# One step of a hybrid decoder layer on one core: keys and values turned by VectorE instead of TensorE, twelve gate tiles ahead of the attention, one more pair of the mixer by halves, value products moved behind the next transposes

## The chip, the cores and the metric

The kernel runs on one core of a Trainium2 chip. The metric is the device time of one execution in microseconds (us). Three executions of the kernel before took 1712.73, 1715.70 and 1717.58 us; the median is 1715.7 us. A further execution was recorded by the hardware profiler; all rows below are from that one.

## The reference, cut to what matters

One decoder layer is computed for 1024 prompt tokens and for 8 sequences of 4 new tokens each (1056 token columns together; every activation is kept transposed, features on the partitions, tokens on the free axis). All data are 32 bit floats.

- `h = RMSNorm(x)`, and one combined projection `h @ w_in` gives, among other things, the queries, keys and values of the attention (512 columns each) and the two gates `g_A` and `g_B` (1024 columns each).
- Branch A is stick-breaking attention, 8 heads of 64: `s = sigmoid(q.k/8 + bias)` under a strictly causal mask, weight `w = s * (product of 1 - s over all later keys)`, output `w @ v`.
- Branch B is a gated delta rule, 4 heads of 128, evaluated in chunks (called GDN below), a serial chain per head.
- Merge: `sigmoid(g_A) * (o_A @ w_pa) + sigmoid(g_B) * (o_B @ w_pb)`, then `w_o`, then the residual.
- Channel mixer: `x + relu(RMSNorm(x) @ w_up)^2 @ w_down`, hidden width 4096, that is 32 tiles of 128 features.
- The prompt's new keys and values are outputs too, in token order: `new_k_prompt` and `new_v_prompt`, pages of 128 tokens by 8 heads by 64.

## The kernel before, in words

A dense product is three matrix products in a fast 32 bit format: every operand is split by ScalarE and VectorE into a high and a low part, and `dense` (lines 134 to 139) issues high*high, high*low and low*high for each 128 rows of depth. A tile is 128 features by up to 288 token columns. Transposes by TensorE and the value products of the attention are issued in the full 32 bit format instead, and TensorE goes back and forth between the two.

Instructions are placed by a planner that simulates the engines: the program's order is a priority, `tc.issue_after(ins)` keeps what follows behind an instruction, `tc.high_priority()` puts it ahead. Each engine then executes its own list strictly in order. DMAs are issued from SP's list, except a few that GpSimd (POOL in the profile) or ScalarE issues; an issue waits in its engine's list until what it reads is there.

The stages, in order of time:

1. Norm and transposes of the input.
2. GDN heads (`gdn_head`), with the projections of queries, keys and values (lines 793 to 831) and the first gate tiles used by the planner as work between the steps of the serial chain. For each of four pairs of heads `p` and for keys and values, the projected tile `f` (128 features by 1024 tokens) is turned into token order by eight TensorE transposes (`tr8`, `tr` on line 111) into two PSUM banks, copied by ScalarE to `nt` (line 819) and stored by SP to the output (line 821); the values are stored a second time to the scratch tensor `v_d` (line 823). The tiles `f`, `hi`, `lo`, `nt` and later the gate tiles `gt` share four buffers (`NFT = 4`). GpSimd has steps of every GDN head: masks of `E` (lines 430, 432) and `tv` (457, 458), powers (`rpow`, line 114).
3. Attention of the 8 new-token sequences, whose cached pages are gathered by GpSimd DMAs (lines 599, 612).
4. The attention of the prompt in 64 blocks (head, 128 queries). `scores` makes a block's `s`, GpSimd masks it and forms `1 - s` (lines 951, 954), VectorE runs the scan and the product (958, 959). `stage_b` issues, four blocks later, the block's transposes (`transposed`, line 962), then some fill work, then `values_of`. For heads 0 to 5 the value product takes two blocks at once, each into one half of the partitions, and the loop over key tiles alternates between the two blocks. The first product needs the first block's weights alone. Until block 34 (`SPLIT`) the fill work is what is left of the 16 gate tiles (`gjobs`, 11 before the attention and 5 in it, four steps each) and nine steps that write a transposed copy of x (`residual_step`); after it, the product with `w_pb`.
5. Merge, `w_o`, second norm.
6. Mixer, first half. With `NF = 16`, hidden tiles `f` and `f + 16` are a pair; 13 pairs (`f` from 3) are combined to seven blocks and stored for the second half (`hc_d`), and pairs 0 to 2 are stored as they are (`h_d`). `up_products` makes a pair with seven half-depth products; `up_plain` makes one tile directly and is used for pairs 0 to 2 in the first half of the tokens.
7. Mixer, second half, in three groups of pairs, [3..6], [7..10] and [11..15] (line 1538 ff.): seven products per pair (`pw`, 168 matrix instructions a pair), each with its own split of the loaded `hc` (`load_h`) and of the weights (`weight_part`). The first group's first loads are issued by GpSimd.
8. The six plain tiles (`fl`) are multiplied directly (`pv`, 96 matrix instructions a tile), beside the final norm and the output.

## Time and profile before

| | |
|---|---|
| time, median of 3 runs | 1715.7 us (1712.73 to 1717.58) |
| the profiled execution's own time | 1713.05 us |
| its span in the trace | 1711.3 us |
| granted TensorE clock, mean | 0.997 |
| VectorE busy | 1155.2 us |
| ScalarE busy | 774.3 us |
| GpSimd busy | 207.3 us |

The span runs from the first to the last recorded instruction; 1.75 us of the execution lie around it. PE is TensorE's matrix work, PEld its weight loads, DVE VectorE, ACT ScalarE, POOL GpSimd, SP the engine that issues most DMAs. Matrix instructions are pipelined: the recorded length of one is more than its distance to the next, so the distance is read from the number of instructions in a stretch in which PE is busy throughout.

### The profile page before, as it was taken

How to read it: one execution, taken by the hardware profiler on the slowest of the kernel's cores; microseconds unless marked ns; L12 is line 12 of the kernel's file. 1: busy time of each engine (PE TensorE's matmuls, PEld its weight loads, DVE VectorE, ACT ScalarE, POOL GpSimd, SP SyncE). 2: the span in 40 equal slices, each digit the busy share in tenths (PEclk: the TensorE clock that was granted, in tenths of full speed). 3: DMA queues.
4: the chain of work that ended last, by engine and by line, in shares of the span. 5: the costliest groups of instructions: out<-in, count | busy, mean ns of one | idle time of the engine just before them, and what ended most of it. 6: DMA issues, size and time to landing. Idle time of an engine off the chain costs nothing.

```text
span 1711.3 us, 34643 instructions
## 1 busy us (share of the span) xinstructions
PE 1676.0 (98%) x13958; PEld 1620.3 (95%) x13958; DVE 1155.2 (68%) x2317; ACT 774.3 (45%) x1542; POOL 207.3 (12%) x243
## 2 busy tenths in 40 slices
PE   6999999999999999999999999999999999999998
PEld 6999999999999799988999999999999999999998
DVE  6656676877325337779766578877777679788843
ACT  5453434343324225565433356544444564444353
POOL 1110111110004225345300000000000000000000
PEclk9999999999999999999999999999999999999999
DMA  5132233244537577876134645554443766433421
GB/s 181 38 118 81 69 95 103 73 124 134 152 96 233 156 202 181 201 211 189 44 126 132 176 132 150 160 160 145 139 139 125 268 216 214 144 118 96 133 78 62
DMA packets 259036, 239.24 MB, mean 140 GB/s; under 512 B 55890, under 2 KB 217011, under 8 KB 258876
## 3 DMA queue, kind: packets, MB, share of 16 engines
q1 hardware_dynamic: 253926, 226.27, 44.0%
q0 software_dynamic: 3200, 10.52, 2.0%
q8 instruction: 110, 1.80, 0.4%
q10 hardware_dynamic: 1750, 0.23, 0.1%
q14 instruction: 50, 0.41, 0.1%
HBM read 163.21 MB, written 73.77 MB: 138 GB/s over the span
## 4 chain that ended last, share of the span: by engine, by line
PE 88%; DVE 4%; DMA 4%; issue 2%; ACT 2%; SPq 0%; POOL 0%; DVEq 0%; POOLq 0%; ACTq 0%
PE pu L139 6%; PE pu L137 6%; PE pu L138 6%; PE pw L139 5%; PE pw L138 5%; PE pw L137 5%; PE pd_g L137 4%; PE pd_g L138 4%; PE pd_g L139 4%; PE wt L111 2%; PE po L996 2%; PE px L138 1%; PE px L137 1%; PE px L139 1%; PE pv L139 1%
## 5 line engine op out<-in xcount | busy, mean ns | idle before, releaser
L139 PE MATMUL pu<-Xh,ul 128*128 128x264 f32 x812 | 230.1, 284 | 0.0
L137 PE MATMUL pu<-Xh,uh 128*128 128x264 f32 x812 | 229.8, 283 | 0.1
L138 PE MATMUL pu<-Xl,uh 128*128 128x264 f32 x812 | 229.7, 283 | 0.0
L137 PE MATMUL pw<-hc,w 128*128 128x264 f32 x728 | 204.1, 284 | 2.4 <-ACT w L1490 2.4
L138 PE MATMUL pw<-hc,w 128*128 128x264 f32 x728 | 204.6, 285 | 0.0
L139 PE MATMUL pw<-hc,w 128*128 128x264 f32 x728 | 200.8, 285 | 1.0 <-DVE w L1491 1.0
L137 PEld LDWEIGHTS pu<-Xh,uh 128*128 128x128 f32 x812 | 153.1, 189 | 0.3 <-ACT uh L1241 0.3
L138 PEld LDWEIGHTS pu<-Xl,uh 128*128 128x128 f32 x812 | 152.7, 188 | 0.0
L139 PEld LDWEIGHTS pu<-Xh,ul 128*128 128x128 f32 x812 | 152.0, 188 | 0.0
L138 PE MATMUL pd_g<-xl,wh_g 128*128 128x256 f32 (+1 forms) x512 | 149.4, 292 | 0.0
L137 PE MATMUL pd_g<-xh,wh_g 128*128 128x256 f32 (+1 forms) x512 | 149.3, 292 | 0.0
L139 PE MATMUL pd_g<-xh,wl_g 128*128 128x256 f32 (+1 forms) x512 | 148.5, 290 | 0.0
L137 PEld LDWEIGHTS pw<-hc,w 128*128 128x128 f32 x728 | 136.8, 188 | 2.6 <-ACT w L1490 2.6
L138 PEld LDWEIGHTS pw<-hc,w 128*128 128x128 f32 x728 | 136.2, 188 | 0.0
L139 PEld LDWEIGHTS pw<-hc,w 128*128 128x128 f32 x728 | 134.4, 188 | 1.4 <-DVE w L1491 1.4
L958 DVE TENSOR_TENSOR_SCAN pr<-am 128x127 f32<-128x127 f32 (+7 forms) x64 | 89.0, 1393 | 30.1 <-POOL am L954 30.1
L137 PEld LDWEIGHTS pd_g<-xh,wh_g 128*128 128x128 f32 x512 | 97.1, 190 | 3.2 <-issue 2.5
L138 PEld LDWEIGHTS pd_g<-xl,wh_g 128*128 128x128 f32 x512 | 97.1, 190 | 2.7 <-issue 2.4
L139 PEld LDWEIGHTS pd_g<-xh,wl_g 128*128 128x128 f32 x512 | 97.0, 189 | 2.0 <-issue 1.8
L1490 ACT ACTIVATE w<-a 128x512 fp32r<-128x512 f32 x78 | 43.4, 620 | 90.3 <-PE pw L139 80.1
L139 PE MATMUL px<-mh,wl_wo 128*128 128x264 f32 x256 | 72.2, 285 | 1.3 <-DVE wl_wo L1242 1.2
L138 PE MATMUL px<-ml,wh_wo 128*128 128x264 f32 x256 | 72.6, 285 | 0.0
(578 smaller groups left out, 5069.0 us busy)
## 6 DMA issues: line engine op xcount, KB each, us to landing
hc_d<-t SPq DMA_DIRECT2D x26, 924.0 KB
hc<-hc_d SPq DMA_DIRECT2D x87, 264.0 KB
a<-in_w_down_dram SPq DMA_DIRECT2D x48, 256.0 KB
ws_g<-in_w_in_dram SPq DMA_DIRECT2D x16, 512.0 KB
ws_wo<-in_w_o_dram SPq DMA_DIRECT2D x32, 256.0 KB
ua<-in_w_up_dram SPq DMA_DIRECT2D x16, 512.0 KB
ub<-in_w_up_dram SPq DMA_DIRECT2D x16, 512.0 KB
gA_d<-gt SPq DMA_DIRECT2D x8, 528.0 KB
```

Source lines behind the costliest of these rows:

```text
L111: PE.transpose(out, in_, ident[:k, :k])
L137: PE.matmul(pt[:, :n], lhsT=wh[k], rhs=xh[k], start=(k == 0), stop=False)
L138: PE.matmul(pt[:, :n], lhsT=wh[k], rhs=xl[k], start=False, stop=False)
L139: PE.matmul(pt[:, :n], lhsT=wl[k], rhs=xh[k], start=False, stop=(k == nk - 1))
L958: V.tensor_tensor_scan(pr[:, n - 1:0:-1], am_r, am_r, 1.0, op0=ALU.mult, op1=ALU.bypass)
L996: PE.matmul(po[64 * r:64 * r + 64, 0:P], lhsT=vn[:, b, rs], rhs=wts[hh, 2 * m + r][:, b * P:(b + 1) * P], start=(b == 0), stop=(b == 2 * m ...
L1490: S_.activation(tl[:, 0], src, AF.Copy)
```

## The change

- New keys and values: the transposes of TensorE and ScalarE's copies go. VectorE's `transpose` transposes every 32 by 32 square of `f` within its place (one instruction over 128 by 1024), and GpSimd issues four DMAs that put the squares where they belong in a scratch tensor `n_d` in token order: each moves 1024 pieces of 128 bytes. A fifth GpSimd DMA copies the scratch tensor to the output, 1024 pieces of 512 bytes, and has to wait for the four. `v_d` and its store go; the attention reads `n_d["v"]`.
- Gates: 12 tiles ahead of the attention instead of 11, 4 in it; a gate's weights are fetched when the split of the tile before has been issued (`fetch_w`). The nine residual steps are on consecutive fill steps, 3 to 11.
- Attention: block `x - 1`'s value product is issued behind block `x`'s last transpose instead of at the end of its own stage. `wt` has three buffers instead of two, `pr` one instead of two.
- Mixer: 14 pairs by halves (`f` from 2) and 4 plain tiles; `up_plain` makes a pair and, for pair 2, the combined blocks. The first half has as many matrix instructions as before. Groups are [2..5], [6..10] and [11..15]. The first group's first weight splits have high priority.

```diff
+    n_d = {x: dr.tile([4, NP, P], F32, name=f"n{x}_d") for x in "kv"}
...
+    ahead_w = {}
+    def fetch_w(col):
+        ahead_w[col] = wpool.tile([P, 8, P], F32, tag="wst", name=f"ws_c{col}", bufs=1)
+        SY.dma_start(ahead_w[col], winv[:, :, col:col + P])
...
-                ws.append(load_w(winv[:, :, col:col + P], name))
+                if col not in ahead_w:
+                    fetch_w(col)
+                ws.append(load_w(None, name, st=ahead_w[col]))
+                if next_col is not None:
+                    fetch_w(next_col)
...
-                for hf, pt in enumerate(tr8(f, f"n{nm}{p}", lambda n_: dtile(n_, True))):
-                    S_.activation(nt[:, hf * 512:(hf + 1) * 512], pt, AF.Copy)
+                V.transpose(nt, f[:, 0:NP])
+                for a in range(4):
+                    G.dma_start(n_d[nm][p].rearrange("(b i) f -> i b f", i=32)[:, :, 32 * a:32 * a + 32],
+                                nt[32 * a:32 * a + 32].rearrange("i (b j) -> i b j", j=32))
                 dst = nk_prompt if nm == "k" else nv_prompt
-                SY.dma_start(dst[0, 0, :, :, 2 * p:2 * p + 2, :].rearrange("c t h d -> t c (h d)"), c8(nt))
-                if nm == "v":
-                    SY.dma_start(v_d[p], c8(nt))
+                G.dma_start(dst[0, 0, :, :, 2 * p:2 * p + 2, :].rearrange("c t h d -> (c t) (h d)"), n_d[nm][p])
...
-            wts[blks[x]] = transposed(blks[x], state[x][0])
+            wts[blks[x]], last = transposed(blks[x], state[x][0])
+        if x:
+            with tc.issue_after(last.ins):
+                values_of(blks[x - 1])
         for f in fill:
             f()
-        values_of(blks[x])
+        if x == NB - 1:
+            values_of(blks[x])
...
-    for j, b in gjobs[:11]:
+    for j, b in gjobs[:12]:
...
-            if t % 2 == 1 and t >= 3:
-                fills.append(lambda t=(t - 3) // 2: residual_step(t))
+            if 3 <= t < 12:
+                fills.append(lambda t=t - 3: residual_step(t))
...
-    NPL = 3
+    NPU, NPL = 3, 2
...
-    groups = [list(range(3, 7)), list(range(7, 11)), list(range(11, 16))]
+    groups = [list(range(2, 6)), list(range(6, 11)), list(range(11, 16))]
...
-            ws = [weight_part(q, f, i) for q, f in zip(qs2, fs)]
+            with tc.high_priority() if gi == i == 0 else ExitStack():
+                ws = [weight_part(q, f, i) for q, f in zip(qs2, fs)]
```

## Rows read from the trace of the kernel before

**Rows 1.** The page: busy time of the engines, and the chain of waits by engine.
```profile
PE 1676.0 (98%) x13958; PEld 1620.3 (95%) x13958; DVE 1155.2 (68%) x2317; ACT 774.3 (45%) x1542; POOL 207.3 (12%) x243
...
PE 88%; DVE 4%; DMA 4%; issue 2%; ACT 2%; SPq 0%; POOL 0%; DVEq 0%; POOLq 0%; ACTq 0%
```

**Rows 2.** Busy time by stretch; columns as the first line names them.
```profile
core 0: us, PE busy (x) PEld busy (x) DVE busy (x) ACT busy (x) POOL busy (x), PEclk, DMA share, GB/s
160.00:460.00 300.00, 295.63 (x2702) 289.12 (x2701) 206.21 (x524) 123.04 (x293) 32.14 (x29) 1.00 0.38 113
635.00:755.00 120.00, 119.99 (x985) 108.22 (x984) 86.06 (x79) 63.13 (x139) 51.19 (x66) 1.00 0.78 183
755.00:795.00 40.00, 39.09 (x306) 32.00 (x304) 37.36 (x37) 25.16 (x50) 27.06 (x24) 1.00 0.94 278
1200.00:1220.00 20.00, 20.00 (x167) 20.00 (x166) 14.47 (x33) 9.40 (x17) 0.00 (x0) 1.00 0.46 148
```

**Rows 3.** PE, new keys and values: group by form (busy, mean ns, idle), chain pieces (start, length).
```profile
L111 PE MATMUL t_nv<-ident,vf 128*128 128x128 f32 x32 | 5.0, 278 | 0.0
L111 PE MATMUL t_nk<-ident,kf 128*128 128x128 f32 x32 | 4.9, 276 | 1.7 <-ACT ntk L819 1.7
...
23.52 0.87 PE xtp L111 x8
```

**Rows 4.** PE in order of time, value products and neighbours: start, length, instructions.
```profile
640.11 0.43 PE L996 MATMUL po<-wt,vn 128*64 128x128 f32 x2
...
708.78 0.43 PE L996 MATMUL po<-wt,vn 128*64 128x128 f32 x2
709.15 0.39 PE L138 MATMUL pd_g<-xl,wh_g 128*128 128x256 f32 x1
...
849.53 1.09 PE L1010 MATMUL po<-wt,vn 128*64 128x128 f32 x16
850.55 0.44 PE L111 MATMUL wt<-ident,s 128*128 128x128 f32 x2
...
854.70 0.43 PE L1010 MATMUL po<-wt,vn 128*64 128x128 f32 x2
```

**Rows 5.** PE, products of the mixer's second half, by form: busy, mean ns, idle before.
```profile
L137 PE MATMUL pw<-hc,w 128*128 128x264 f32 x728 | 204.1, 284 | 2.4 <-ACT w L1490 2.4
...
L137 PE MATMUL pv<-hp,wd 128*128 128x264 f32 x192 | 55.1, 287 | 0.2 <-ACT wd L1598 0.2
```

**Rows 6.** The chain of waits between the mixer's halves: start, length, what.
```profile
1350.82 0.65 ACT t L1405
1351.52 0.52 issue
1352.04 0.62 ACT w L1490
```

**Rows 7.** VectorE and ScalarE by form: busy, mean ns of one, idle before.
```profile
L1063 DVE STREAM_TRANSPOSE xs<-xr 128x1024 f32<-128x1024 f32 x8 | 9.9, 1236 | 10.7 <-DMA xr<-in_x_prompt_dram 6.8 <-DMA gA_d<-gt 4.0
L1413 DVE TENSOR_TENSOR t<-t 128x264 f32<-128x264 f32 x26 | 11.0, 423 | 0.0
...
L819 ACT ACTIVATE ntk<-t_nk 128x512 f32<-128x512 f32 x8 | 4.8, 598 | 0.1
```

**Rows 8.** GpSimd by form, its DMA issues and gathers: busy, mean ns, idle before.
```profile
L599 POOL DMA_INDIRECT kg<-in_cache_k_dram,idx x16 | 17.7, 1105 | 39.0 <-PE dkt L111 25.2 <-DVE sel L845 6.8 <-DMA kg<-in_cache_k_dram,idx 2.6
L1476 POOL DMA_DIRECT2D a<-in_w_down_dram x4 | 2.2, 538 | 0.3
```

**Rows 9.** GpSimd in order of time around one GDN head: start, length, idle before.
```profile
241.23 2.17 POOL L430 TENSOR_SCALAR_AFFINE_SELECT E<-E 128x1024 f32<-128x1024 f32 x1 [17.69 <-PE o L556]
243.47 1.09 POOL L432 TENSOR_SCALAR_AFFINE_SELECT E<-E 128x1024 f32<-128x1024 f32 x1
245.13 0.21 POOL L362 COPY zs<-z 128x32 f32<-128x32 f32 x1 [0.57 <-ACT z L361]
252.60 2.59 POOL L114 TENSOR_TENSOR f<-f,powc 128x8 f32<-128x8 f32 x1 [7.25 <-DVE f L568]
```

**Rows 10.** SP's issues of the transposed copy of x: ns min/median/max, first and last start.
```profile
L1066 SPq DMA_DIRECT2D xT_d<-xs x33: 303/563/3272, 647.8 to 748.0; - x33
```

More of the change, by code (lines that the diff above doesn't have):

```diff
@@ L110, in tr @@
     def tr(out, in_, k=P):
-        PE.transpose(out, in_, ident[:k, :k])
+        return PE.transpose(out, in_, ident[:k, :k])
     def rpow(out, in_, which, n):
@@ L150, in hybrid_step @@
     k_d = [dr.tile([4, P, NP], F32, name=f"k{x}_d") for x in "hl"]
-    v_d = dr.tile([4, P, NC, P], F32, name="v_d")
+    n_d = {x: dr.tile([4, NP, P], F32, name=f"n{x}_d") for x in "kv"}
     cg_d = dr.tile([GH, NC, P], F32, name="cg_d")
@@ L954, in scores @@
         G.tensor_scalar(am[:, :n], s[:, :n], -1.0, 1.0, op0=ALU.mult, op1=ALU.add)
-        pr = ak.tile([P, NP], F32, tag="pr", name=f"pr{hh}_{i}")
+        pr = ak.tile([P, NP], F32, tag="pr", name=f"pr{hh}_{i}", bufs=1)
         am_r = am[:, n - 1:0:-1]
@@ L963, in transposed @@
         hh, i = blk
-        wt = ak.tile([P, NP], F32, tag="wt", name=f"wt{hh}_{i}", bufs=2)
+        wt = ak.tile([P, NP], F32, tag="wt", name=f"wt{hh}_{i}", bufs=3)
         for b0 in range(0, i + 1, 4):
@@ L968, in transposed @@
             for b in range(bn):
-                tr(pt[:, b * P:(b + 1) * P], s[:, (b0 + b) * P:(b0 + b + 1) * P])
+                last = tr(pt[:, b * P:(b + 1) * P], s[:, (b0 + b) * P:(b0 + b + 1) * P])
             S_.activation(wt[:, b0 * P:(b0 + bn) * P], pt[:, :bn * P], AF.Copy)
-        return wt
+        return wt, last
     heads, vns, oTs, wts = {0: head0}, {}, {}, {}
@@ L1053, in ev, with col @@
                 S_.activation(gt[:, o:o + n], pt[:, :n], AF.Sigmoid)
-        return proj_steps(3592 + b * D + j * P, f"g{b}_{j}", ev, lambda: SY.dma_start((gA_d, gB_d)[b][j], gt))
+        def col(j, b):
+            return 3592 + b * D + j * P
+        return proj_steps(col(j, b), f"g{b}_{j}", ev, lambda: SY.dma_start((gA_d, gB_d)[b][j], gt),
+                          None if (j, b) == (KT - 1, 1) else col(*((j, 1) if b == 0 else (j + 1, 0))))
     def residual_step(t):
@@ L1083, in hybrid_step @@
     fills = []
-    for x, (j, b) in enumerate(gjobs[11:]):
+    for x, (j, b) in enumerate(gjobs[12:]):
         for c in range(len(CX)):
@@ L1341, in next_bank, with combos @@
         return mk4[bank[0] % 4](name)
-    def up_plain(f, g):
-        wh, wl = load_8(wuv[:, :, f * P:(f + 1) * P], f"up{f}")
-        t = up_.tile([P, 7, QN], F32, tag="t", name=f"tp{f}{g}")[:, 0:2]
-        for h, (i, ii) in enumerate(((0, 1), (7, 6))):
-            pt = next_bank(f"pu{f}{g}_{h}")
-            dense(pt, wh, wl, [Xh[g][i][:, k] for k in range(4)] + [Xh[g][ii][:, k] for k in range(4)],
-                  [Xl[g][i][:, k] for k in range(4)] + [Xl[g][ii][:, k] for k in range(4)], QN)
-            S_.activation(t[:, h], pt[:, :QN], AF.Relu)
-        S_.activation(t, t, AF.Square)
-        SY.dma_start(by_group(h_d[f], g), t)
+    def combos(f, g, t):
+        V.tensor_tensor(t[:, 4], t[:, 3], t[:, 0], op=ALU.subtract)
+        V.tensor_tensor(t[:, 3], t[:, 6], t[:, 3], op=ALU.subtract)
+        V.tensor_tensor(t[:, 2], t[:, 6], t[:, 4], op=ALU.subtract)
+        V.tensor_tensor(t[:, 5], t[:, 2], t[:, 1], op=ALU.subtract)
+        SY.dma_start(hc_d[f - NPL, :, :, g * QN:(g + 1) * QN].rearrange("i p n -> p i n"), t)
+    def up_plain(f, g):
+        t = up_.tile([P, 7, QN], F32, tag="t", name=f"tp{f}{g}")
+        rows = (t[:, 0:4:3], t[:, 1:7:5])
+        for r in range(2):
+            wh, wl = load_8(wuv[:, :, (f + NF * r) * P:(f + NF * r + 1) * P], f"up{f}{r}")
+            for h, (i, ii) in enumerate(((0, 1), (7, 6))):
+                pt = next_bank(f"pu{f}{g}{r}_{h}")
+                dense(pt, wh, wl, [Xh[g][i][:, k] for k in range(4)] + [Xh[g][ii][:, k] for k in range(4)],
+                      [Xl[g][i][:, k] for k in range(4)] + [Xl[g][ii][:, k] for k in range(4)], QN)
+                S_.activation(rows[r][:, h], pt[:, :QN], AF.Relu)
+            S_.activation(rows[r], rows[r], AF.Square)
+            if f < NPL:
+                SY.dma_start(by_group(h_d[f + NF * r], g), rows[r])
+        if f >= NPL:
+            combos(f, g, t)
     def up_weights(f):
@@ L1430, in hybrid_step @@
     norm(1)
-    for f in range(NPL):
+    for f in range(NPU):
         up_plain(f, 0)
-        up_plain(f + NF, 0)
     kxctx.close()
     u7a = pool("u7a", stack=uctx)
-    for f in range(NPL, NF):
+    for f in range(NPU, NF):
         w7 = up_weights(f)
```

14 lines of the change are left out of this document (5 added, 9 removed).

## Prediction, made before the changed kernel was run

> **What bounds the kernel now.** I read the page's busy times and its chain of waits first, then busy time by stretch, then the groups of PE by form. TensorE is busy for 1676.0 of 1711.3 us and holds 88% of the chain that ended last [rows 1]. Busy alone would not prove it, because recorded lengths overlap, so look at the pace: in a quiet stretch PE has 167 instructions of 264 columns in 20 us [rows 2], 0.120 us from one to the next although each is recorded with 0.284 us [rows 5]. The stretch of the GDN heads, 160 to 460 us, has 295.6 us of PE in 300, and the first part of the attention, 635 to 755 us, 119.99 in 120; VectorE has 206 and 86 us there [rows 2]. So an instruction taken from TensorE is worth its distance to the next one, and work put on the other engines costs nothing until one of them, in order, holds up TensorE. The one stretch with a second bound is 755 to 795 us, just behind block 34: VectorE is busy for 37.4 of 40 us and the DMA engines for 0.94 [rows 2].
>
> **Keys and values.** Removed: 64 transposes of TensorE. The nearest row for their pace is eight transposes that take 0.87 us, 0.109 us each [rows 3]; 64 by 0.109 is 7.0 us. The two groups' busy time, 4.9 + 5.0 = 9.9 us [rows 3], is the upper end, since the last of each piece overlaps what follows. TensorE also waited 1.7 us for ScalarE's copies out of PSUM [rows 3]; no other wait stands behind those, as the transposes that wrote those banks are gone. Taken: 7.0 + 1.7 = 8.7 us. ScalarE loses 16 copies of 0.6 us [rows 7], on no path here.
>
> Added: eight VectorE transposes over 128 by 1024, 1.24 us each [rows 7], 9.9 us in all against 94 us in which VectorE idles between 160 and 460 us [rows 2]. They take the place of nothing on the chain; if one stands ahead of a GDN step, that step is 1.24 us late and TensorE has projections in hand. Cost: nothing; 8 x 1.24 = 10 us if that cover were gone every time.
>
> Added on GpSimd: 32 scatters of 1024 pieces and 8 copies of 1024 pieces. No row shows such a DMA from GpSimd. The cheap end is the 0.54 us of an issue with 128 rows [rows 8], 40 x 0.54 = 22 us in all. The dear end by piece count is eight times that, 4.3 us, 172 us in all; by the gathers' 1.1 us for 128 rows [rows 8] it would be 8.8 us and 354 us. SP's issues of exactly this shape, 1024 pieces of 128 bytes, have a median of 0.56 us [rows 10], but they are not made by GpSimd. I take 4.3 us, from the row nearest in kind, scaled by pieces. GpSimd has 32 us of work between 160 and 460 us [rows 2], so the amount fits. The order is the question: GpSimd executes in order, a batch of four scatters would hold it for 17 us, and the copy behind them waits until they have landed. Queued behind a batch can be a GDN step that is worth 0.2 to 2.6 us by itself, such as the masks of E or the power of f [rows 9]; behind that mask VectorE and TensorE wait, for that head. The planner knows of the waits and has projections and gate tiles to put between, and PE idles only 4.4 us in those 300. I charge 4 us (one short batch caught in the open); the ends are 0 and 30 us, the latter if three heads each lose about half a batch twice.
>
> The Trainium skill, in "DMA: Bandwidth & Descriptors", section "SWDGE vs HWDGE vs iDMA", says that a DMA issued by GpSimd has its descriptors computed in software, one pair for each operation, and the table of issuing engines on that page puts simple stores on SP instead. This speaks for the dear end and against this change. Its section "Anatomy of one DMA" says on the other hand that many descriptors can be emitted before the cost shows, by which the sum would be the one with no charge, 4 us less. The row of 0.54 us has 128 rows and decides neither.
>
> SP loses 8 output stores and 4 stores of v; the attention's loads of v are read in pieces of 512 bytes instead of whole rows, which the DMA engines, at 0.78 in the attention's first part [rows 2], still fit. The buffer `nt` is held until GpSimd's scatters have read it, longer than before; four buffers on, a projection's tile waits for it. At 17 us a batch that is about one projection's length (96 matrix instructions at 0.12 us, 11.5 us) and a half, so I count nothing, but it belongs to the 30 us end.
>
> **Value products.** The same instructions are issued, so what can go is the price of breaking them up. In the timeline of PE, 29 value products start with a piece of exactly two instructions, the first at 640.11 us and the last at 854.70 us: the first block's weights are there, the second's are still being copied. Such a piece costs 0.37 us until the next instruction (708.78 to 709.15) [rows 4], and the rest of the product does not get shorter by it: a piece of 16 takes 1.02 us (849.53 to 850.55) [rows 4], 0.064 us an instruction, three times less than in the piece of two. With both blocks' weights there and the products behind the next transposes, in the same number format, the piece of two should vanish in its run: 29 x 0.36 = 10.4 us. Six of the 29 lie between 755 and 795 us, where VectorE has 2.6 us to spare in 40 [rows 2]; I don't count these, 23 x 0.36 = 8.3 us. The other end is 0: the planner breaks them elsewhere.
>
> **Gates.** One tile (96 matrix instructions, 11.5 us) moves from the fill work to the time ahead of the attention: TensorE does it once in either place. The list of PE's waits has none for a gate's weights, so fetching them earlier is worth nothing. What goes from the attention's first part is cover: with the gate tile and the pieces gone, 635 to 795 us shrinks from 160 to some 141 us, while VectorE keeps 86 + 37 - 1 = 122 us and the DMA engines 0.78 x 120 + 0.94 x 40 = 131 us of work [rows 2]. Both fit; DMA at 131 of 141 is the tight one, and three buffers of `wt` and one of `pr` change nothing of it (scan and product follow each other on VectorE). Cost: nothing, with 8.3 us as the other end.
>
> **Mixer.** `pv` falls from 576 (3 x 192 [rows 5]) to 384 instructions and `pw` rises from 2184 (3 x 728) to 14 x 168 = 2352: 24 fewer, at 0.120 us 2.9 us. VectorE gets 8 combining operations more (0.42 us each [rows 7], 3.4 us) in a half where it is busy for 14.5 of 20 us [rows 2]. A group of five pairs is what the last group is already, so its prefetch is known to hold. Between the halves TensorE waits 2.4 us for the first weights' split [rows 5]; in the chain ScalarE does another tile's Relu for 0.65 us and 0.52 us pass in issue before it [rows 6]. High priority takes away that much, 1.2 us; the ends are 0 and 2.4.
>
> **Sum.** 8.7 + 8.3 + 2.9 + 1.2 = 21.1 us gained, 4 us charged: 17 us. From the profiled execution's 1713.05 us that is 1696 us. The median of the runs shown is 2.65 us above that execution, by which the same 17 us end at 1698.7; the forecast for a median is 1698 us.
>
> **Rivals.**
> - GpSimd holds up the GDN heads (slower). Place: 160 to 460 us; mechanism: a head's masks and powers stand behind a batch of descriptors, and TensorE's list, fixed in advance, stands at that head's next product. For it: the GpSimd steps of head 1 fall on 241 to 253 us [rows 9], where values of the first pair are ready as well; in-order issue. Against it: 268 us of idle GpSimd in 300 [rows 2]. It decides from 21 us of stalls on. At the gathers' price per row a batch is 35 us; three heads losing 15 us each give 45 us: 1715.7 - 21 + 45 = 1740 us. Chance 0.10. The Trainium skill's "SBUF — State Buffer" adds that VectorE in some modes locks GpSimd out while it writes descriptors; no row here shows a scatter under that.
> - The same, but small: stalls of 12 to 25 us eat the gain, 1715.7 within 5 us. Chance 0.10.
> - The attention gives nothing back: VectorE's scans or the DMA engines become the bound in 635 to 795 us, or the products stay broken up. For it: VectorE at 37.4 of 40 us behind block 34; against it: 34 us of idle VectorE in the 120 before. 17 - 8 = 9 us gained: 1707 us. Chance 0.18.
> - More than counted: no charge on GpSimd (4), all 29 pieces (2), the transposes at their busy time (3), the whole wait between the halves (1) and the GDN stretch's remaining 2.7 us of waits: 1698 - 13 = 1685 us. Chance 0.20.
>
> The forecast as worked out has 0.42. Within 0.3% (5 us, about what a measurement of this kernel can tell from no change) is the second rival; faster by more than that has the forecast, the third and the fourth, 0.80; slower 0.10. The range of 8 in 10 goes from the fourth rival with 3 us of run-to-run spread, 1682, to the lower part of the second, 1713.
>
> **What would show it.** The groups of TensorE for turned keys and values gone, and VectorE with eight more transposes of 1.24 us; GpSimd's new DMA issues with their length (0.5, 4 or 9 us decides the first two rivals) and PE's busy time between 160 and 460 us against the clock; value products of 14, 22, 30 instructions in one piece, none of two; 2352 `pw` and 384 `pv`; PE's wait for the first weights under 1.3 us. The prediction is wrong if GDN products wait for GpSimd, or if PE idles for several us in the attention with VectorE or a load as the releaser.

## The result, and the profile after

Ten timed executions of the changed kernel have a median of 1721.1 us (1715.2 to 1728.3). Ten of the kernel before, on the same chip, have 1716.0 us (1711.2 to 1717.6). The ratio measured over these executions is 1.0039, with a 95% interval of 1.0022 to 1.0055 (the medians by themselves give 1.0030): slower by 5 to 7 us, where 17 us faster was forecast. The profiled execution took 1719.18 us, with a span of 1717.5 us.

The page of the changed kernel, busy times and chain of waits by engine, answers to [rows 1]:
```profile
PE 1660.1 (97%) x13870; PEld 1612.4 (94%) x13870; DVE 1180.6 (69%) x2343; ACT 772.1 (45%) x1535; POOL 258.0 (15%) x283
...
PE 81%; DMA 7%; DVE 5%; issue 2%; SPq 2%; ACT 2%; POOL 0%; DVEq 0%; POOLq 0%; ACTq 0%
```
TensorE is busy for 16 us less, and yet the span is 6 us longer. So it stands idle for 57.4 us (1717.5 - 1660.1) in place of 35.3. The chain says the same: PE fell from 88% to 81%, and DMA rose from 4% to 7%.

Busy time by stretch after the change, in the stretches of [rows 2]:
```profile
core 0: us, PE busy (x) PEld busy (x) DVE busy (x) ACT busy (x) POOL busy (x), PEclk, DMA share, GB/s
160.00:460.00 300.00, 290.69 (x2610) 285.10 (x2609) 209.39 (x519) 110.17 (x269) 64.15 (x68) 0.98 0.42 119
635.00:755.00 120.00, 111.79 (x947) 102.53 (x940) 87.09 (x78) 62.27 (x137) 63.28 (x67) 0.97 0.88 196
755.00:795.00 40.00, 31.17 (x261) 27.14 (x257) 36.14 (x40) 19.18 (x40) 21.93 (x24) 0.91 0.81 244
1200.00:1220.00 20.00, 20.00 (x168) 20.00 (x167) 14.46 (x33) 9.71 (x17) 0.00 (x0) 1.00 0.46 145
```
The mixer's stretch (the last row) is as it was. The loss is in two places: the GDN heads (9.3 us idle in 300, before 4.4) and the attention (8.2 and 8.8 us idle, before nothing and 0.9). In both, the granted clock, PEclk, is below 1. Over the whole span the ten executions have a mean granted clock of 0.984 to 0.992, each lower than the 0.997 of the kernel before in its profiled execution.

For finer stretches, first TensorE in the kernel before, then in the changed one (stretch, busy time, granted clock, DMA share):
```profile
340.00:480.00 140.00, 137.16 (x1257) 1.00 0.46 137
480.00:700.00 220.00, 219.99 (x1864) 0.99 0.65 176
700.00:800.00 100.00, 98.25 (x788) 1.00 0.83 214
800.00:960.00 160.00, 159.05 (x1242) 1.00 0.37 113
```
```profile
340.00:480.00 140.00, 131.91 (x1173) 0.95 0.51 143
480.00:700.00 220.00, 218.98 (x1889) 1.00 0.63 166
700.00:800.00 100.00, 83.06 (x691) 0.93 0.85 216
800.00:960.00 160.00, 156.25 (x1230) 1.00 0.39 114
```
These rows give an account that I use from here on. **Idle** is the stretch minus PE's busy time. **Half clock** is half of the time in which PE was busy while its granted clock was at the lower level (PEclk is the mean: 1 at 2.4 GHz, 0.5 at 1.2). What is left of the span is **work**. Before: 1711.3 = 35.3 idle + 3.4 half clock + 1672.6 work. After: 1717.5 = 57.4 + 12.0 + 1648.1. The work fell by 24.5 us. Of the 21.1 us that were forecast, 18.2 are work (7.0 + 8.3 + 2.9) and the rest are waits. It was all given back, and 6 us more: 22.1 in idle TensorE and 8.6 in half clock. The price of the half clock in this account is a definition, but the runs support it: over 277 executions of all kernels below and of the kernel before, each compared with the others of its own kernel on its chip, a microsecond lost by the mean granted clock goes with some 0.8 us of time (an estimate by a straight line).

How a wait becomes half clock can be followed at one GDN head. VectorE's list in the kernel before (start, length, line, operation, idle before it and what ended it):
```profile
341.25 0.74 DVE L347 TENSOR_SCALAR cvq<-upq,vec 128x1024 f32<-128x1024 f32 x1
342.07 1.66 DVE L572 TENSOR_SCALAR nw<-nw,f 128x128 f32<-128x128 f32 x8
343.64 2.60 DVE L349 SCALAR_TENSOR_TENSOR cvq<-upq,vec,cvq 128x1024 f32<-128x1024 f32 x2
346.16 1.40 DVE L575 SCALAR_TENSOR_TENSOR zl<-zl,vec,t_o 128x512 f32<-128x512 f32 x2
348.64 1.25 DVE L484 STREAM_TRANSPOSE U<-t 128x1024 f32<-128x1024 f32 x1 [1.08 <-DMA t<-tv_d]
```
The same place in the changed kernel:
```profile
340.89 0.74 DVE L357 TENSOR_SCALAR cvq<-upq,vec 128x1024 f32<-128x1024 f32 x1
345.52 1.25 DVE L494 STREAM_TRANSPOSE U<-t 128x1024 f32<-128x1024 f32 x1 [3.89 <-DMA t<-tv_d]
346.69 1.61 DVE L582 TENSOR_SCALAR nw<-nw,f 128x128 f32<-128x128 f32 x8
348.22 1.28 DVE L359 SCALAR_TENSOR_TENSOR cvq<-upq,vec,cvq 128x1024 f32<-128x1024 f32 x1
349.42 1.22 DVE L128 TENSOR_TENSOR wl_ak<-ws_ak,wh_ak 128x1024 fp32r<-128x1024 f32 x1
350.55 0.18 DVE L823 COPY vsT<-pd_av 128x32 f32<-128x32 f32 x1
350.65 1.23 DVE L829 STREAM_TRANSPOSE ntv<-vf 128x1024 f32<-128x1024 f32 x1
```
And TensorE there, with what it waited for:
```profile
346.99 1.70 PE L111 MATMUL t_o<-ident,nw 128*128 128x128 f32 x8 [2.46 <-DVE nw L582]
350.79 0.58 PE L137 MATMUL pd_aq<-xh,wh_aq 128*128 128x256 f32 x1 [2.10 <-DVE vsT L823]
```
Before, the list has `nw`, `cvq` and `zl` ahead of `U`, which needs a round trip through DRAM, and VectorE waits 1.08 us for it. In the changed list `U` comes first. VectorE stands for 3.89 us, and `nw` and the copy `vsT`, which frees a PSUM bank, are queued behind it; once it is over they follow without a wait of their own. TensorE waits 2.46 and 2.10 us for these two, and the granted clock behind them shows the rest:
```profile
344.00:349.00 5.00, 2.23 (x13) 1.00 0.05 11
349.00:356.00 7.00, 5.21 (x24) 0.51 0.59 149
356.00:363.00 7.00, 7.00 (x107) 1.00 0.60 153
```
At 446 us it is the same: `U` waits 4.78 us, TensorE 2.08 us, and the clock is at half from 448.0 to 454.8 us. First VectorE, then TensorE:
```profile
446.12 1.25 DVE L494 STREAM_TRANSPOSE U<-t 128x1024 f32<-128x1024 f32 x1 [4.78 <-DMA t<-tv_d]
```
```profile
448.14 1.06 PE L503 MATMUL l<-U,E 32*32 32x32 f32 x32 [2.08 <-DVE zl L585]
```

### The profile page after: what moved, and what is told of

The parts are those of the page before. It is cut to its first block, busy times and chain, and to the rows that moved or that the text cites. A ratio compares the mean times of both kernels' runs of the same rounds, so it can differ in the third digit from the quotient of the medians.

```text
span 1717.5 us, 34592 instructions
## 1 busy us (share of the span) xinstructions
PE 1660.1 (97%) x13870; PEld 1612.4 (94%) x13870; DVE 1180.6 (69%) x2343; ACT 772.1 (45%) x1535; POOL 258.0 (15%) x283
## 4 chain that ended last, share of the span: by engine, by line
PE 81%; DMA 7%; DVE 5%; issue 2%; SPq 2%; ACT 2%; POOL 0%; DVEq 0%; POOLq 0%; ACTq 0%
PE pu L139 6%; PE pu L137 6%; PE pu L138 6%; PE pw L139 5%; PE pw L138 5%; PE pw L137 5%; PE pd_g L139 3%; PE pd_g L137 3%; PE pd_g L138 3%; PE px L139 1%; PE px L138 1%; DMA xr<-in_x_prompt_dram 1%; PE px L137 1%; PE wt L111 1%; SPq L1086 1%
## 5 line engine op out<-in xcount | busy, mean ns | idle before, releaser
L137 PE MATMUL pw<-hc,w 128*128 128x264 f32 x784 | 220.5, 285 | 2.4 <-ACT w L1518 2.4
L138 PE MATMUL pw<-hc,w 128*128 128x264 f32 x784 | 220.1, 286 | 0.0
L139 PE MATMUL pw<-hc,w 128*128 128x264 f32 x784 | 215.7, 286 | 1.0 <-DVE w L1519 1.0
L137 PEld LDWEIGHTS pw<-hc,w 128*128 128x128 f32 x784 | 148.0, 189 | 2.6 <-ACT w L1518 2.6
L138 PEld LDWEIGHTS pw<-hc,w 128*128 128x128 f32 x784 | 147.1, 189 | 0.0
L139 PEld LDWEIGHTS pw<-hc,w 128*128 128x128 f32 x784 | 145.3, 190 | 1.4 <-DVE w L1519 1.4
L965 POOL TENSOR_SCALAR am<-s 128x128 f32<-128x128 f32 (+7 forms) x64 | 75.7, 1183 | 35.1 <-DVE pr L969 29.6
L1491 ACT ACTIVATE hc<-hc 128x528 fp32r<-128x528 f32 x98 | 61.6, 643 | 26.3 <-DMA hc<-hc_d 24.7
```

The source lines that it names most:

```text
L137: PE.matmul(pt[:, :n], lhsT=wh[k], rhs=xh[k], start=(k == 0), stop=False)
L138: PE.matmul(pt[:, :n], lhsT=wh[k], rhs=xl[k], start=False, stop=False)
L139: PE.matmul(pt[:, :n], lhsT=wl[k], rhs=xh[k], start=False, stop=(k == nk - 1))
L965: G.tensor_scalar(am[:, :n], s[:, :n], -1.0, 1.0, op0=ALU.mult, op1=ALU.add)
L1491: S_.activation(tl[:, 0], tl[:, 1].bitcast(F32), AF.Copy)
```

## The experiments

Every kernel was timed in 6 to 12 executions against the kernel before, on the same chip in each group. In the table, "340", "480" and "700" are idle + half clock of TensorE in the profiled execution at 340 to 480, 480 to 700 and 700 to 960 us. The ratios with their intervals are taken over all executions of a run; a quotient of the medians differs from them by up to 0.0014, and microseconds worked out from a ratio share its interval. The three columns are of one execution each, which need not be a typical one: that of e3 was the slowest of its ten, that of e2 the second fastest. Runs that are compared with each other across groups (e5 with e13, e8 with e10) were timed on different chips, each against the kernel before on its own.

```
run                   ratio [95%]               340        480        700
before                1                       2.8+0.0    0.0+1.7    2.6+0.0
the whole change      1.0039 [1.0022, 1.0055]  8.1+5.8    1.0+0.0   20.7+4.4
e1  gates             1.0012 [0.9995, 1.0028]  2.8+0.0    0.0+0.0    7.2+3.4
e2  values            0.9976 [0.9950, 1.0003]  2.8+0.0    0.1+0.0    5.2+1.7
e3  keys/values       1.0038 [1.0017, 1.0059]  7.0+4.4    2.4+6.8    6.7+2.6
e4  mixer             0.9977 [0.9958, 0.9997]  2.8+0.0    1.1+6.8    2.6+0.0
e5  VectorE, old DMA  1.0045 [1.0028, 1.0062]  4.0+1.7   11.0+7.9    6.4+2.7
e6  PE, new DMA       1.0021 [1.0007, 1.0035]  4.4+0.0    6.0+3.4    2.5+0.0
e7  v in whole rows   1.0034 [1.0020, 1.0048]  9.1+3.2    4.5+6.8    6.7+3.3
e8  values+mixer      0.9929 [0.9910, 0.9949]  2.9+0.0    5.1+0.0    6.8+0.0
e9  all but keys/val. 0.9970 [0.9956, 0.9984]  3.2+0.0    4.3+1.7   11.9+2.2
e10 all but gates     1.0058 [1.0042, 1.0075]  7.6+4.6    6.4+3.3   18.2+7.7
e11 all+64 transposes 1.0011 [0.9998, 1.0024]  4.8+0.0    4.5+0.0   14.4+4.4
e12 residual spread   1.0050 [1.0038, 1.0062]  8.4+4.2    4.1+0.0   18.7+6.5
e13 no turning        0.9973 [0.9959, 0.9987]  1.3+0.0    4.8+1.7    4.3+3.1
e14 both turnings     1.0100 [1.0082, 1.0119] 12.1+5.8    1.0+1.7    2.5+0.0
e15 e8+early weights  0.9953 [0.9935, 0.9972]  2.8+0.0    0.0+0.0    6.0+1.6
e16 short VectorE     1.0029 [1.0018, 1.0040]  6.4+1.7    4.3+3.4    2.6+0.0
e17 VectorE behind    1.0019 [1.0005, 1.0034]  7.0+1.7    5.1+0.0    4.0+1.7
e18 e9, spread        0.9957 [0.9943, 0.9972]  2.8+0.0    4.8+3.3    8.1+4.7
```

**Which part loses (e1 to e4).** Each part alone on the kernel before. The gates part, twelve tiles in front, weights one tile ahead, nine residual steps in a row:
```
-    for j, b in gjobs[:11]:
+    for j, b in gjobs[:12]:
...
-            if t % 2 == 1 and t >= 3:
-                fills.append(lambda t=(t - 3) // 2: residual_step(t))
+            if 3 <= t < 12:
+                fills.append(lambda t=t - 3: residual_step(t))
```


> The kernel before with the gate part of the change alone: 12 gate tiles in front, weights fetched a tile ahead, the nine residual steps on consecutive fill steps. Theory A (VectorE stands in order at a residual step's transpose and waits for the load of x, which has one buffer and is issued nine times in close succession): slower by 10 to 20 us, VectorE waiting about 20 us for xr between 640 and 800 us, where it waited 6.8 before. Rival B (the moved value products made the attention late): no change, within 3 us. Rival C (the GDN stretch alone carries the loss): no change here either, and no idle PE in the attention.

The value products alone:
```
+        if x:
+            with tc.issue_after(last.ins):
+                values_of(blks[x - 1])
         for f in fill:
             f()
-        values_of(blks[x])
+        if x == NB - 1:
+            values_of(blks[x])
```


> The kernel before with the value products behind the next block's transposes alone. Theory A: faster by 6 to 10 us, pieces of two gone. Rival B: slower or no faster, with PE waiting for VectorE's products or for weights' copies in the attention. Rival C says nothing of it: faster by 6 to 10 us.

The keys and values alone:
```
-                for hf, pt in enumerate(tr8(f, f"n{nm}{p}", lambda n_: dtile(n_, True))):
-                    S_.activation(nt[:, hf * 512:(hf + 1) * 512], pt, AF.Copy)
+                V.transpose(nt, f[:, 0:NP])
+                for a in range(4):
+                    G.dma_start(...)
```


> The kernel before with keys and values turned by VectorE and scattered by GpSimd alone. Theory A: the stalls of the GDN stretch (about 7 us of waits and two drops of the granted clock, worth 3.4 us each) belong to this part, so it gains 8.7 and loses some 10 to 14: 1 to 5 us slower, stalls near 345 and 445 us. Rival C, in its strong form: 10 us slower or more. Rival D (the GDN stalls come from the whole plan having shifted, not from this part): 7 to 9 us faster.

The mixer and the priority alone:
```
-    NPL = 3
+    NPU, NPL = 3, 2
```


> The kernel before with the mixer's part alone (14 pairs by halves, 4 plain tiles, priority for the first weight splits). All theories: 3 to 4 us faster, with 24 matrix instructions fewer; the 2.4 us wait for the first weights' split is still there in the changed kernel, so priority is expected to give 0 of its 1.2.

Measured, against a median of 1713.7 us: gates 1715.8, values 1709.7, keys and values 1722.5, mixer 1709.0 us. The gates part alone is no loss, so VectorE's waits for the residual's loads are not the cause as a property of that part; the values in their new place are no loss either. The keys and values carry the loss: 6.5 us by the ratio (8.8 by the medians), where 8.7 less 4 were to be won. The product of the four ratios is 1.0003, and the whole is 1.0039. That some 6 us come from the parts together is not shown by this, since the intervals of the four together are wider; the runs below look at it.

**Engines or way to memory (e5 to e7).** VectorE's transposes with SyncE's old stores; TensorE's transposes with GpSimd's new way; and the keys and values part with v laid into whole rows again. The core of each diff, the first two against the kernel before, the third against e3:
```
-                for hf, pt in enumerate(tr8(f, f"n{nm}{p}", lambda n_: dtile(n_, True))):
-                    S_.activation(nt[:, hf * 512:(hf + 1) * 512], pt, AF.Copy)
+                V.transpose(nt, f[:, 0:NP])
```


> The kernel before, with VectorE's transposes of the new keys and values in place of the 64 matrix transposes and 16 copies of ScalarE, but with the old way to memory: SyncE stores them and the scratch copy of the values in whole rows, and GpSimd issues nothing. (Left out: the 32x32 blocks are not put in their places, so rows of the new keys and values are permuted.) The keys and values part alone measured 1722.5 us, ratio 1.0038. Theory P (the loss lies on the engines: without the 64 transposes TensorE has less to lay over the GDN heads, waits for VectorE at 340 to 480 us and falls to half clock there): about the same loss, ratio 1.002 to 1.005. Theory M (the loss lies in the way to memory: GpSimd's queue, the round trip, the values read back in 512-byte pieces when the attention starts): the transposes' 7.0 us come through, ratio 0.995 to 0.998.


```
+                G.dma_start(n_d[nm][p].rearrange("(c t) f -> t c f", t=P), c8(nt))
+                G.dma_start(dst[...].rearrange("c t h d -> (c t) (h d)"), n_d[nm][p])
```


> The kernel before, with its 64 matrix transposes and ScalarE's copies kept, but with the new way to memory: GpSimd issues a store of the turned tile into a scratch of rows and then a copy of it to the output, and the attention reads the values back from that scratch in 512-byte pieces. Theory P: no change, ratio 0.999 to 1.001. Theory M: the whole loss without the transposes' gain, ratio 1.004 to 1.009 (8 to 15 us).


```
+                if nm == "v":
+                    G.dma_start(v_d[p], n_d[nm][p].rearrange("(c t) f -> t c f", t=P))
...
-        SY.dma_start(vn, n_d["v"][p].rearrange("(c t) f -> t c f", t=P))
+        SY.dma_start(vn, v_d[p])
```


> The keys and values part alone, with a further DMA by GpSimd behind each copy that lays the values into a scratch of whole 4096-byte rows, from which the attention reads them as in the kernel before; it moves the 512-byte pieces from the start of the attention to the projections at 220 to 450 us. Theory M in its narrow form (the attention's loads are held up by the values' 512-byte reads): better than 1.0038, ratio 0.997 to 1.001. Theory P, or theory M through GpSimd's queue: no better, ratio 1.003 to 1.006.

With the old way to memory the loss is whole (1.0045); the new way with TensorE's transposes costs 1.0021, some 4 us; reading v in whole rows mends nothing (1.0034). So the loss lies mostly on the engines, theory P. The narrow form of theory M is refuted. Beside TensorE's transposes the way to memory has a smaller price of its own, more than theory P allowed; beside VectorE's none shows (1.0038 with it, 1.0045 without).

**The parts together (e8 to e12).** Values and mixer; the change without keys and values; without gates; with 64 unused transposes on TensorE; with the residual steps spread. The last two are the only ones with new lines:
```
+                for pt in tr8(f, f"n{nm}{p}", lambda n_: dtile(n_, True)):
+                    pass
                 V.transpose(nt, f[:, 0:NP])
```
```
+    RS = (3, 4, 6, 7, 9, 10, 12, 13, 15)
...
-            if 3 <= t < 12:
-                fills.append(lambda t=t - 3: residual_step(t))
+            if t in RS:
+                fills.append(lambda t=RS.index(t): residual_step(t))
```


> The kernel before with the value products and the mixer part alone, the two that were faster by themselves (0.9976 and 0.9977). If they add up: ratio 0.9953, about 1705.7 us. If each is only the same better order of the last stages: 0.997 to 0.998.

> The changed kernel without its keys and values part: value products, mixer and gates, and the 64 matrix transposes as before. Theory F (the transposes are the work that covers the GDN heads' waits, and everything that comes earlier by them is paid again as idle TensorE and half clock): the two gains stay, ratio 0.992 to 0.996 (value products and mixer alone gave 0.9929), idle TensorE at 340 to 480 us near 3 us as before. Theory G (the gates part and the shorter value products together leave the attention without work, keys or not): 700 to 800 us as idle as in the changed kernel (16.9 us), ratio 0.998 to 1.002.

> The changed kernel without its gates part: keys and values, value products, mixer. Theory F: the loss of the keys and values part stays whatever the gates do: 0.9929 with 0.0038 to 0.0060 more, so 0.996 to 1.000, idle and half clock at 340 to 480 us as in the changed kernel (8.1 and 5.8 us). Theory G: the attention is as it was in the kernel with value products and mixer alone (idle 5.4 us at 700 to 800), and most of the loss of the whole change against it is gone: 0.993 to 0.996.

> The changed kernel with the 64 matrix transposes of the new keys and values put back on TensorE, their results unused (no copy, no wait behind them): 7.0 us more work for TensorE and nothing less. Theory F: they fill idle places: the time is that of the changed kernel or below (ratio to the kernel before 1.000 to 1.005, TensorE idle and half clock together down by 7 us or more from 69.4). If TensorE's work were what sets the end: 7 us above the changed kernel, ratio 1.007 to 1.009.

> The changed kernel with its nine residual steps spread over the attention's gate tiles (steps 3, 4, 6, 7, 9, 10, 12, 13, 15) in place of nine in a row. Theory A (VectorE stands 20 us at the residual transposes for their loads, in a row, and the attention waits for VectorE): VectorE's wait for xr falls to below 10 us, idle TensorE at 700 to 800 us from 16.9 to below 10, ratio 0.998 to 1.001. Theory G (the attention is short of work for TensorE): idle stays above 13, ratio 1.002 to 1.005.

Values and mixer together have 0.9929: 1709.7 against 1722.0 us, the gain in full. The keys and values turn 0.9970 into 1.0039 with the gates part (e9, whole change) and 0.9929 into 1.0058 without it (e8, e10): a loss of 12 and 22 us whatever the gates do, as theory F had it, though 1.0058 is more than it allowed and 0.9970 lies between the two theories. Theory G is refuted for the gates part by itself, since without it the attention is as idle (18.2 + 7.7). But the attention does lose by the combination: at 700 to 960 us 6.8 us idle and half clock with values and mixer, 14.1 with the gates, 25.1 with keys and values as well.

The 64 transposes put back on TensorE cost nothing: 1.0011 against 1.0039, with intervals that just overlap. TensorE of that kernel at 340 to 480 and 700 to 800 us:
```profile
340.00:480.00 140.00, 135.19 (x1237) 1.00 0.46 135
...
700.00:800.00 100.00, 89.06 (x741) 0.95 0.91 224
```
They fill what stood idle (8.1 us became 4.8, 16.9 became 10.9). So in the changed kernel TensorE's work is no longer what sets the end in these two places. Spreading the residual steps helped nothing, and VectorE's wait for them did not shrink; first the changed kernel, then the spread one (waits of VectorE at 640 to 870 us: total, times, longest):
```profile
DVE xs L1083 <- DMA xr<-in_x_prompt_dram: 20.1, 7, 5.5
```
```profile
DVE xs L1083 <- DMA xr<-in_x_prompt_dram: 21.1, 7, 6.8
```
So spreading the steps does not take the wait away here, and theory A, that the row of nine makes it, finds no support.

**Who makes the GDN heads wait (e13, e14).** Four corners: TensorE's transposes yes or no, VectorE's yes or no. No turning at all, and both:
```
-                for hf, pt in enumerate(tr8(f, f"n{nm}{p}", lambda n_: dtile(n_, True))):
-                    S_.activation(nt[:, hf * 512:(hf + 1) * 512], pt, AF.Copy)
...
+                SY.dma_start(..., c8(f[:, 0:NP] if nm == "v" else hi.bitcast(F32)))
```


> The kernel before without any turning of the new keys and values: SyncE stores the unturned tiles to the output and the scratch, by the old way. (Left out: the transposes, on any engine; the attention and the outputs then use unturned keys and values.) Theory F (cover): the 7.0 us of matrix transposes and ScalarE's copies are gone and nothing has come in their place, and the time still does not fall: ratio 0.999 to 1.005, idle TensorE and half clock together above 50 us (38.8 in the kernel before, 62.6 with VectorE's transposes). Theory V (what loses is VectorE's eight transposes, 9.9 us in its order between the GDN heads' operations): the whole gain shows, ratio 0.994 to 0.997, idle and half clock near 40.


```
+                V.transpose(nt, f[:, 0:NP])
                 for hf, pt in enumerate(tr8(f, f"n{nm}{p}", lambda n_: dtile(n_, True))):
```


> The kernel before with VectorE's eight transposes of the new keys and values added ahead of the matrix transposes, whose copies then overwrite the result: VectorE has 9.9 us more work there and TensorE none less. Theory F: no change, ratio 0.999 to 1.002. Theory V: the whole loss, without the gain of 7 us: ratio 1.005 to 1.010.

With TensorE's transposes alone 1 (the kernel before), with none 0.9973, with VectorE's alone 1.0045, with both 1.0100. Theory F falls as the cause: without TensorE's transposes, and without anything in their place, the kernel is 4.6 us faster (interval 2 to 7), though it has lost the same cover. Theory V comes nearer, but 0.9973 is not its whole gain. VectorE's eight transposes cost 0.72% where TensorE's are gone, 12 us (e5 against e13, some 9 to 16 by the intervals; e13 also has no `nt` tile in the shared buffers), and 17 us where they stand (e14; 16 by the medians). TensorE at 340 to 480 us, first without turning, then with both:
```profile
340.00:480.00 140.00, 138.68 (x1274) 1.00 0.44 134
```
```profile
340.00:480.00 140.00, 127.94 (x1130) 0.95 0.40 125
```
VectorE's waits in its own list for the heads' round trips through DRAM at 200 to 480 us, in the run with both (total, times, longest):
```profile
DVE cgb L481 <- ACT cgb L480: 20.4, 3, 10.8
...
DVE ob L464 <- DMA ms<-ms_d: 7.9, 3, 3.3
...
DVE U L484 <- DMA t<-tv_d: 2.3, 2, 1.2
```
That is 30.6 us where the kernel before has 12.6 (5.3, 1.9 and 5.4), the changed kernel 23.4, and the one without turning 14.5 (`cgb` itself waits for ScalarE, which waits for a load).

But e5, with VectorE's transposes and the old DMAs, has only 15.0 us of these waits (7.9, 3.9 and 3.2), about as many as e13. TensorE of its profiled execution:
```profile
340.00:480.00 140.00, 136.01 (x1237) 0.99 0.45 137
480.00:700.00 220.00, 209.02 (x1684) 0.96 0.57 157
```
It loses 5.7 us at the heads and 18.9 us behind them, at 480 to 700 us (e13: 1.3 and 6.5). So the waits at the heads account for e14 and for a part of the whole change, and not for most of the 12 us between e5 and e13. What makes the stretch behind the heads slower in e5 is open.

**Length or order (e16, e17).** Eight short transposes in the same places, and eight full ones of which neither TensorE nor ScalarE waits for any directly (the buffer `nt` is still held by them):
```
+                V.transpose(nt[:, 0:32], f[:, 0:32])
                 for hf, pt in enumerate(tr8(f, f"n{nm}{p}", lambda n_: dtile(n_, True))):
```


> The kernel before with eight small VectorE transposes (128x32 in place of 128x1024) ahead of the matrix transposes, whose copies overwrite them: the same places in VectorE's list and the same waits of ScalarE's copies as with the full ones (ratio 1.0100), but only some 0.2 us each in place of 1.23. If the loss is the time that VectorE's list is longer there: ratio 0.999 to 1.003. If it is the wait that couples ScalarE's copies and the matrix transposes to VectorE's list, whatever its length: 1.006 to 1.012.


```
                     S_.activation(nt[:, hf * 512:(hf + 1) * 512], pt, AF.Copy)
+                V.transpose(nt, f[:, 0:NP])
```


> The kernel before with the eight full VectorE transposes behind ScalarE's copies, over their result (left out: the order within 32x32 blocks, as the stored keys and values are then turned by VectorE alone without the blocks being put in place). Nothing of TensorE or ScalarE waits for VectorE's transposes any more, only SyncE's stores. If 9.9 us more in VectorE's list make the loss (the GDN heads' operations and the copies that free PSUM come later, and the planner puts the list in another order): ratio 1.004 to 1.010. If only the coupled copies of the run before made it: 0.999 to 1.002.

The short ones add some 1.6 us to VectorE's list and cost 1.0029, 5 us; the full ones add 9.9 us and cost 1.0019 there, 3 us. The first lies within what length alone was to give (0.999 to 1.003), the second within what coupling alone was to give (0.999 to 1.002), so neither by itself makes the 17 us of e14; length and coupling together do. In the coupled place 8 us more of transposes cost 12 us more (e16 against e14). Coupled copies are not needed for a loss, though, since e5 has none and loses 12 us against e13. At 340 to 480 us TensorE loses 8.1 and 8.7 us in these two runs where the kernel before loses 2.8.

All these runs have a new list. Of the 531 operations of VectorE at 160 to 480 us in the kernel before, 420 stand in the same order in the changed kernel (the longest common sequence, the new transposes left out), 419 to 433 in e3, e5, e14, e16 and e17, and 517 or more in the runs that leave the transposes as they were (e1, e2, e4, e6, e8, e9). But the list of e13 is just as new (421), and e13 is faster. So a new list by itself is not the loss.

**The gates' halves (e15, e18).** Values and mixer with the early weights alone, and e9 with its residual steps spread:
```
+                if next_col is not None:
+                    fetch_w(next_col)
```


> Value products and mixer (0.9929 by themselves) with the half of the gates part that loads each gate tile's weights one tile ahead, but 11 tiles in front and the residual steps as before. With the whole gates part it was 0.997. If the early loads cost (they compete with the attention's), about 0.997 again; if the twelfth tile in front and the nine residual steps in a row do, 0.992 to 0.994.

> Value products, mixer, weights fetched one tile ahead and 12 gate tiles in front, with the nine residual steps spread (3, 4, 6, 7, 9, 10, 12, 13, 15). The same with nine in a row gave 0.997, with 11 tiles in front and the old residual steps 0.9953. If the row of residual steps costs: 0.993 to 0.996 and VectorE's wait for xr at 640 to 870 us below 10 us. If the twelfth tile in front does: 0.997 to 0.999.

0.9953 and 0.9957, with the whole part 0.9970, without any of it 0.9929. The neighbours' intervals overlap, so the halves are not told apart. One sign speaks for the row of residual steps: VectorE's wait for `xr` at 640 to 870 us is 5.9 us in e18 and 10.5 in e9, as the expectation had it. Both kernels e8 (1709.7 us against 1722.0) and e15 (1704.8 against 1714.3) beat the kernel before and the changed one; which of the two is better is open.

## Why the prediction was wrong

**Keys and values: the step that failed is "Cost: nothing".** I set VectorE's eight transposes against 94 us of idle VectorE and wrote "TensorE has projections in hand". They were not free in any pair: 12 us in place of TensorE's (e13 against e5), 17 us ahead of them (e14), 3 us where no copy waits for them (e17). The first two reach or pass the 10 us that I gave for no cover at all. The idle sum was the wrong measure. VectorE's list is in order, and between its operations stand round trips of the heads. In the changed kernel VectorE stands in front of such a round trip, and TensorE, whose list is fixed as well, stands at the head's next product or at a PSUM bank that VectorE frees. Then the half clock comes on top, which no term of mine had: 8.6 us in the whole change. In the changed kernel and in e14 this is shown by their rows. It is not the whole cause: e5 loses most behind the heads, and e13 has as new a list without a loss. Why the planner puts `U` first is open, and so is what the 12 us of e5 against e13 consist of.

The Trainium skill, in "VectorE: DVE Perf Modes", section "Rules for kernel authors", puts a 128 by 128 transpose on TensorE where its result may go to PSUM, and only one inside 32 by 32 blocks on VectorE. These runs agree for this kernel: by the four corners TensorE is better by some 8 us (1.0045 against 1, interval 5 to 11).

The gain was too large too. Without the transposes, their copies and anything in their place the kernel wins 4.6 us (2 to 7) of my 8.7.

**GpSimd: the price was wrong, the charge by chance about right.** GpSimd's issues in the changed kernel, by line (busy, mean ns of one, idle before and for what):
```profile
L831 POOL DMA_DIRECT2D nk_d<-ntk x16 | 12.8, 805 | 27.4 <-DVE ob L474 21.0 <-DVE ntk L829 3.5 <-DVE kb L541 2.9
L831 POOL DMA_DIRECT2D nv_d<-ntv x16 | 12.6, 792 | 35.4 <-DVE ntv L829 19.4 <-DVE ob L474 12.9 <-DVE tv L476 3.1
...
L834 POOL DMA_DIRECT2D out_dram<-nk_d x4 | 3.2, 800 | 16.8 <-DMA nk_d<-ntk 16.8
...
L834 POOL DMA_DIRECT2D out_dram<-nv_d x4 | 3.1, 778 | 17.2 <-DMA nv_d<-ntv 17.2
```
A scatter of 1024 pieces takes GpSimd 0.8 us, not 4.3: eight times the rows of [rows 8] took half as long again. Scaling by pieces was the error. The Trainium skill's section "Anatomy of one DMA" in "DMA: Bandwidth & Descriptors", that many descriptors come before the cost shows, fits this; the dear end, for which I cited the section "SWDGE vs HWDGE vs iDMA", does not. No scatter took longer than 1.02 us, so nothing held one up for long. GpSimd does stand for 34 us before the copies until the scatters have landed. But at 160 to 480 us TensorE waits for no step of GpSimd, and VectorE for 0.8 us (before 1.0), so no direct wait of the heads for it shows. The new way costs 0.21%, 4 us (e6, interval 1 to 6); through which wait is open. The first rival's mechanism, a batch of 17 or 35 us, did not happen. The second rival, small stalls by GpSimd, named a time near the one that came (1715.7 within 5 us), but its mechanism did not happen either.

**Value products: sized right as far as shown.** Pieces of two instructions fell from 29 to 7 (22 fewer, 23 counted; the last of the 29 stands at 864.0 us, not at 854.7). TensorE's work fell by 10.1 us in e2 and the profiled span by 9.2, but that execution was the second fastest of its ten. The median fell by 4.0 (0.9976, 0.9950 to 1.0003), which is not clear of noise by itself. Together with the mixer it fell by 12.3 (0.9929), where 8.3 + 2.9 = 11.2 were forecast. This agrees with the 8.3 us and does not measure them alone.

**Gates: "Both fit" failed, in company.** Alone the part changes nothing measurable, as forecast. In the whole change TensorE is idle for 16.9 of the 100 us at 700 to 800, with VectorE busy for 36 of the 40 us behind 755 and the DMA engines at 0.88 in 635 to 755: the third rival, which I had priced at 8 us. It took place with and without the gates part, wherever keys and values stand beside the value products (25.1 us in the whole change and 25.9 in e10 at 700 to 960, before 2.6). Almost all of the idle time there is TensorE waiting for VectorE (total, times, longest):
```profile
PE wt L111 <- DVE s L970: 9.1, 4, 5.0
PE pb L138 <- DVE obl L1157: 6.4, 1, 6.4
PE pb L137 <- DVE tb L1175: 3.4, 2, 2.5
```
This is the sign that the prediction named for being wrong. Whether VectorE's work or the loads that it waits for end last is not settled: on the chain, loads of `xr` and `ofs` and VectorE's scans alternate (start, length, what):
```profile
720.92 4.10 DMA xr<-in_x_prompt_dram
...
726.28 1.98 DVE pr L969
...
752.82 5.39 DMA ofs<-o_d
```

**Mixer: right; priority: nothing.** The forecast was 2.9 us, measured 0.9977, 4 us with an interval of 0.5 to 7. The products after the change, answering to [rows 5]:
```profile
L137 PE MATMUL pw<-hc,w 128*128 128x264 f32 x784 | 220.5, 285 | 2.4 <-ACT w L1518 2.4
...
L137 PE MATMUL pv<-hp,wd 128*128 128x264 f32 x128 | 36.9, 288 | 0.0
```
2352 and 384, as counted. The wait for the first weights is still 2.4 us: the 1.2 us for the priority were not won.

In sum: the work taken from TensorE was foreseen (18.2 of 24.5 us). What failed is the price, 4 us in the sum and 30.7 us in the trace: 11.1 us at the GDN heads, where I had written "Cost: nothing" for VectorE's transposes, and 22.5 us in the attention, where I had written "Both fit", with some 3 us less elsewhere. By the ratios the keys and values bring 12 us of loss with the gates part and 22 without. How work added at 160 to 460 us makes the attention at 700 us slower is not shown.

## What to carry to other kernels

Where engines run fixed lists, an engine's idle sum does not say that added work is free: look at what stands directly behind it in that list, and at the round trips that the list waits for. Price a stall of TensorE with the half clock that follows it. Expect that an edit among tightly packed heads brings a new list: here every edit of VectorE's or TensorE's transposes moved some hundred of VectorE's 531 operations there, with and without a loss, while edits elsewhere left that list almost as it was. Time the parts of a change alone and in pairs: here two parts had the whole gain (0.9929), and the other two together lost it.

## What the runs showed of the hardware

GpSimd's time for issuing a DMA hardly grows with its pieces: 0.54 us with 128 rows, 0.78 to 0.80 us with 1024.

Half clock followed idle TensorE at 349 us above, but idle TensorE is not needed. In the run with the mixer part alone it came while PE was recorded as busy throughout, with few instructions (41 in 14 us, 93 in the 10 us behind them):
```profile
560.00:570.00 10.00, 10.00 (x62) 1.00 0.63 173
570.00:584.00 14.00, 14.00 (x41) 0.51 0.31 88
584.00:594.00 10.00, 10.00 (x93) 1.00 0.74 215
```
So the price of the half clock does not show as idle time: these 14 us look fully busy. It is no effect of the mixer part: the profiled execution of the kernel before has half clock in the same place, from 573.9 us for 3.4 us, and the mixer part's own executions differ. Seven of its ten have a mean granted clock of 0.997 to 0.998 and three, the profiled one among them, 0.993 or 0.994. So a column of the table above can move by several us from one execution to the next.
